# A decoder layer on one core: the SwiGLU's middle activations transposed by VectorE and moved by GpSimd's transfers

## The chip, the cores and the metric

The kernel runs on one core of a Trainium2 chip. The time is that of one execution on the device in microseconds; several executions are timed and their median is given.

## The reference

One layer with three residual parts over 256 positions of width 2048: a SwiGLU, a mixer (gated linear attention in 4 heads beside dilated attention in 8), and a second SwiGLU. All inputs are float32. The change touches the two SwiGLUs, which are the same but for their weights:

```python
def rms_norm(x, g):
    xf = x.astype(jnp.float32)
    y = xf * lax.rsqrt(jnp.mean(xf * xf, axis=-1, keepdims=True) + EPS)
    return (y * g.astype(jnp.float32)).astype(x.dtype)

def swiglu(x, w_gate, w_up, w_down):
    return (jax.nn.silu(x @ w_gate) * (x @ w_up)) @ w_down

x = x + FFN_RESIDUAL_WEIGHT * swiglu(rms_norm(x, ffn1_norm[l]), ffn1_w_gate[l], ffn1_w_up[l], ffn1_w_down[l])
...
x = x + FFN_RESIDUAL_WEIGHT * swiglu(rms_norm(x, ffn2_norm[l]), ffn2_w_gate[l], ffn2_w_up[l], ffn2_w_down[l])
```

`w_gate` and `w_up` are 2048 x 5632, `w_down` is 5632 x 2048.

## The kernel before

A float32 product is made of three products of rounded operands. `split` (line 87) cuts a tile in two: ScalarE copies it to the type float32r, which is the high part (line 89), and VectorE subtracts that from the tile, which leaves the low part (line 90). Weights become `wh` and `wl`, activations `hh` and `hl` (the normalised input) or `uh` and `ul` (the SwiGLU's middle activations). `products` (line 165) issues high by high (line 171), high by low (line 173) and low by high (line 175), and sums them in PSUM.

Weights come in loads of 1 MB from SyncE's queue (line 148) into one of three buffers `raw`. `prepare` splits each half of a load into a pair `wh`, `wl`, of which there are four buffers (`WBUF`), and `weights` keeps two or three pairs ahead of the matmuls. So the engines of a stage are tied in a ring: TensorE frees a weight buffer, ScalarE and VectorE fill it, VectorE frees the buffer `raw`, SyncE loads the next.

`column_pair` (line 183) is one stage: two blocks of 512 output columns (in the SwiGLU one of the gate and one of the up projection) for both halves of the positions (`t`, 128 each), so four PSUM banks out of six. It goes over the tiles `i` of the inner dimension, 16 in the up-projection and 44 in the down-projection, and for each over `t`; with two column blocks and three products that is 12 matmuls a tile. After the last tile of a half it calls `evac`. Small pieces of work are put in the list `later`, and `column_pair` runs them spread over the steps of the next stage.

In `ffn` (line 218) there are eleven up-projection pairs and then two down-projection pairs. `evac` (line 223) makes the middle activations of 512 columns and 128 positions: ScalarE takes the Silu of the gate (`sg`, line 225), VectorE multiplies it with the up part (`u`, line 226). `u` has positions in its partitions, but the down-projection needs the columns there, so TensorE transposes four squares of 128 into a PSUM bank `tb` (line 229, by the helper's line 85), and `split` writes `uh` and `ul` from that bank (line 230, shown as lines 89 and 90). The call is made twice in a pair, for `t` = 0 and 1.

A scheduler of the framework sets the order in which each engine gets its instructions; an engine then works through its own in that order, and an instruction that waits holds those behind it. GpSimd does small things only: powers for the normalisation (line 106), and loads of constants from its own DMA queue (lines 81 and 298 to 305).

Of the kernel before, what the change touches and what calls it, by code (L numbers as in the profile page):

```python
# [14 lines left out]
F32 = mybir.dt.float32  # L15
# [6 lines left out]
P = 128  # L22
S = 256
D = 2048
# [3 lines left out]
NT = S // P  # L28
# [8 lines left out]
def layer_kernel(tc, x, xT, gains, gla_gate_up, gla_gate_bias, gla_out_norm, att_q_norm, att_k_norm,  # L37
                 w_ff1, w_dn1, w_mix, w_low, w_out, w_ff2, w_dn2, c_sq, c_rope, c_mask, out):

    nc = tc.nc  # L40
# [3 lines left out]
    with ExitStack() as es:  # L44
        cst = es.enter_context(tc.tile_pool(name="cst", bufs=1))
# [7 lines left out]
        def t512(name):  # L53
            return cst.tile([P, 512], F32, name=name, tag="t512", bufs=4)

        def tp_bank():
            return ptp.tile([P, 512], F32, name="tp", tag="tp")


        xs = cst.tile([P, NT * D + 224], F32, name="xs")[:, :NT * D].rearrange("p (t d) -> p t d", t=NT)  # L60
        hh = cst.tile([P, KT, S], F32R, name="hh")
        hl = cst.tile([P, KT, S], F32R, name="hl")
        ident = cst.tile([P, P], F32, name="ident")
# [2 lines left out]
        ss = cst.tile([P, NT, 4], F32, name="ss")  # L66
        ssum = cst.tile([P, NT], F32, name="ssum")
        rt = cst.tile([P, NT], F32, name="rt")
        rq = cst.tile([P, 48], F32, name="rq")[:, :NT]
        junk = cst.tile([P, 512], F32, name="junk")  # L70

        nc.vector.memset(mhalf, -0.5)
# [10 lines left out]
        def transpose(dst, src):  # L83
            n = src.shape[0]
            nc.tensor.transpose(dst, src, ident[:n, :n])  # L85

        def split(dst_h, dst_l, src):

            nc.scalar.activation(dst_h, src, AF.Copy)  # L89
            nc.vector.tensor_sub(dst_l, src, dst_h.bitcast(F32))  # L90
# [71 lines left out]
        def halves(a):  # L162
            return a.rearrange("p (b a) -> p b a", b=2)
# [13 lines left out]
        later = []  # L177
# [5 lines left out]
        def column_pair(acts, evac, span=28, due=None, extra=None, final=False):  # L183

            ps = [None] * NT
            n = len(acts)  # L190
            total = done = 0
            i = 0
            while i < n:
                if i == due:
                    done += len(later)
                    run_later(len(later))
                if extra and i in extra:
                    extra[i]()
                g = WBUF if final and i == n - WBUF else 1
                ws = [weights() for _ in range(g)]  # L200
                for t in range(NT):
                    step = 2 * i + t
                    total = max(total, done + len(later))
                    go = max(-(-total * min(step + 1, span) // span) - done, 0)
                    done += min(go, len(later))
                    run_later(go)
                    if i == 0:
                        ps[t] = [acc_bank(), acc_bank()]
                    last = i + g == n
                    products(ps[t], t, acts[i:i + g], ws, i == 0, last, ((0,), (1,)) if g > 1 else ((0, 1),))  # L210
                    if last:
                        evac(t, [b.rearrange("p (a b) -> p b a", b=2) for b in ps[t]])
                i += g
# [4 lines left out]
        def ffn(name, done, extra=None, final=False):  # L218
            with tc.tile_pool(name=name, bufs=1, reuse_waits="tile") as fp:
                uh = fp.tile([P, FT, S], F32R, name="uh")  # L220
                ul = fp.tile([P, FT, S], F32R, name="ul")
                for b in range(FF // 512):
                    def evac(t, ps, b=b):
                        sg, u = t512("sg"), t512("u")
                        nc.scalar.activation(halves(sg), ps[0], AF.Silu, scale=rt[:, t:t + 1])  # L225
                        nc.vector.scalar_tensor_tensor(halves(u), ps[1], rt[:, t:t + 1], halves(sg), op0=ALU.mult, op1=ALU.mult)  # L226
                        tb = tp_bank()
                        for j in range(4):
                            transpose(tb[:, j * P:(j + 1) * P], u[:, j * P:(j + 1) * P])
                        split(uh[:, 4 * b:4 * b + 4, t * P:(t + 1) * P], ul[:, 4 * b:4 * b + 4, t * P:(t + 1) * P],  # L230
                              tb.rearrange("p (j q) -> p j q", j=4))
                    if b:
                        column_pair(hacts, evac)
                    else:
                        column_pair(hacts, evac, span=16, due=15 if extra else 8, extra=extra)
                for cp in range(2):
                    def evac(t, ps, cp=cp):
                        for j in range(2):
                            c = 2 * cp + j
                            blk = xs[:, t, c * 512:(c + 1) * 512]  # L240
                            nc.vector.scalar_tensor_tensor(halves(blk), ps[j], 0.5, halves(blk), op0=ALU.mult, op1=ALU.add)
                            done(t, c, blk)
                    column_pair([(uh, ul, k) for k in range(FT)], evac, final=final and cp == 1)
# [404 lines left out]
```

## Time and profile before

| what | value |
|---|---|
| median of 3 runs | 1795.85 us (1795.18 to 1795.98) |
| the profiled execution | 1795.97 us |
| its span, first to last instruction | 1794.0 us |
| mean granted TensorE clock, as a share of 2.4 GHz | 0.998 |
| bytes read from memory | 350.35 MB |
| TensorE, VectorE, ScalarE, GpSimd busy | 1783.4, 970.2, 840.6, 28.2 us |

A busy share says how long an engine worked, not whether the kernel waited for it. The chain of waits says that: it is followed back from the last instruction, at each step to what released it. In a timeline a row is an instruction, or several alike in a row, with its start, its duration, and in brackets the idle time before it and what ended that. A matmul's duration overlaps its neighbours', so the time that a matmul costs is read from the distance of starts.

### The profile page before, as it was taken

How to read it: one execution, taken by the hardware profiler on the slowest of the kernel's cores; microseconds unless marked ns; L12 is line 12 of the kernel's file. 1: busy time of each engine (PE TensorE's matmuls, PEld its weight loads, DVE VectorE, ACT ScalarE, POOL GpSimd, SP SyncE). 2: the span in 40 equal slices, each digit the busy share in tenths (PEclk: the TensorE clock that was granted, in tenths of full speed). 3: DMA queues.
4: the chain of work that ended last, by engine and by line, in shares of the span. 5: the costliest groups of instructions: out<-in, count | busy, mean ns of one | idle time of the engine just before them, and what ended most of it. 6: DMA issues, size and time to landing. Idle time of an engine off the chain costs nothing.

```text
span 1794.0 us, 20802 instructions
## 1 busy us (share of the span) xinstructions
PE 1783.4 (99%) x8462; PEld 1553.0 (87%) x8462; DVE 970.2 (54%) x998; ACT 840.6 (47%) x1012; POOL 28.2 (2%) x34
## 2 busy tenths in 40 slices
PE   8999999999999999999999999999999999999999
PEld 7888888888888888888887788888888888888887
DVE  5555555555544645566655666555555555544544
ACT  6444444444444544565753445444444444444342
POOL 0000000000000001011000000000000000000000
PEclk9999999999999999999999999999999999999999
DMA  8555555555555556555444455555555555555653
GB/s 330 190 210 190 207 190 205 193 190 208 199 201 210 188 211 206 195 204 194 165 165 151 153 189 191 208 191 208 189 208 191 207 190 205 194 208 194 232 205 124
DMA packets 52111, 353.79 MB, mean 197 GB/s; under 512 B 5904, under 2 KB 7952, under 8 KB 9776
## 3 DMA queue, kind: packets, MB, share of 16 engines
q1 hardware_dynamic: 48672, 348.15, 53.8%
q10 hardware_dynamic: 2896, 3.17, 0.6%
q0 software_dynamic: 448, 1.15, 0.2%
q8 instruction: 66, 1.08, 0.2%
q14 instruction: 29, 0.24, 0.0%
HBM read 350.35 MB, written 2.10 MB: 196 GB/s over the span
## 4 chain that ended last, share of the span: by engine, by line
PE 99%; ACT 1%; DMA 0%; DVE 0%; issue 0%; ACTq 0%
PE acc L171 32%; PE acc L173 31%; PE acc L175 31%; PE tp L85 2%; PE tp L512 0%; DMA xt<-in_xT_dram 0%; PE tp L378 0%; PE tp L527 0%; PE tp L530 0%; ACT wh L89 0%; ACT L445 0%; PE acc L432 0%; PE acc L433 0%; PE acc L434 0%; PE tp L404 0%
## 5 line engine op out<-in xcount | busy, mean ns | idle before, releaser
L90 DVE TENSOR_TENSOR wl<-raw,wh 128x1024 fp32r<-128x1024 f32 x658 | 802.8, 1224 | 693.6 <-ACT wh L89 693.4
L89 ACT ACTIVATE wh<-raw 128x1024 fp32r<-128x1024 f32 x658 | 691.9, 1055 | 791.1 <-PE acc L175 778.4
L173 PE MATMUL acc<-wl,hh 128*128 128x512 f32 x1792 | 549.2, 382 | 0.0
L175 PE MATMUL acc<-wh,hl 128*128 128x512 f32 x1792 | 543.9, 380 | 0.0
L171 PE MATMUL acc<-wh,hh 128*128 128x512 f32 x1792 | 538.5, 382 | 4.3 <-ACT wh L89 4.3
L171 PEld LDWEIGHTS acc<-wh,hh 128*128 128x128 f32 x1792 | 339.0, 190 | 52.8 <-ACT wh L89 4.6
L175 PEld LDWEIGHTS acc<-wh,hl 128*128 128x128 f32 x1792 | 338.6, 189 | 49.1 <-issue 2.1
L173 PEld LDWEIGHTS acc<-wl,hh 128*128 128x128 f32 x1792 | 338.6, 189 | 49.0 <-issue 2.0
L173 PE MATMUL acc<-wl,uh 128*128 128x512 f32 x704 | 212.6, 379 | 0.0
L175 PE MATMUL acc<-wh,ul 128*128 128x512 f32 x704 | 211.8, 379 | 0.0
L171 PE MATMUL acc<-wh,uh 128*128 128x512 f32 x704 | 210.8, 380 | 0.0
L175 PEld LDWEIGHTS acc<-wh,ul 128*128 128x128 f32 x704 | 133.1, 189 | 18.8
L173 PEld LDWEIGHTS acc<-wl,uh 128*128 128x128 f32 x704 | 133.1, 189 | 18.8
L171 PEld LDWEIGHTS acc<-wh,uh 128*128 128x128 f32 x704 | 133.0, 189 | 18.7
L90 DVE TENSOR_TENSOR ul<-tp,uh 128x512 fp32r<-128x512 f32 x44 | 29.6, 691 | 64.1 <-ACT uh L89 64.1
L89 ACT ACTIVATE uh<-tp 128x512 fp32r<-128x512 f32 x44 | 26.3, 597 | 79.1 <-PE tp L85 77.9
L225 ACT ACTIVATE sg<-acc,rt 128x512 f32<-128x512 f32 x44 | 30.2, 687 | 14.0 <-PE acc L175 13.4
L226 DVE SCALAR_TENSOR_TENSOR u<-acc,rt,sg 128x512 f32<-128x512 f32 x44 | 32.9, 747 | 2.8 <-ACT sg L225 0.4
L85 PE MATMUL tp<-ident,u 128*128 128x128 f32 x176 | 26.4, 273 | 0.0
L85 PEld LDWEIGHTS tp<-ident,u 128*128 128x128 f32 x176 | 22.0, 141 | 3.4
L106 POOL TENSOR_TENSOR rs<-a,mhalf 128x4 f32<-128x4 f32 (+1 forms) x12 | 17.4, 1454 | 278.9 <-DVE a L328 278.9
L171 PE MATMUL acc<-wh,oah 128*128 128x512 f32 x64 | 20.2, 385 | 0.0
(147 smaller groups left out, 558.7 us busy)
## 6 DMA issues: line engine op xcount, KB each, us to landing
raw<-in_w_ff_dram SPq DMA_DIRECT2D x175, 1024.0 KB, 4.8
raw<-in_w_dn_dram SPq DMA_DIRECT2D x88, 1024.0 KB, 4.8
raw<-in_w_mix_dram SPq DMA_DIRECT2D x48, 1024.0 KB, 4.8
raw<-in_w_out_dram SPq DMA_DIRECT2D x16, 1024.0 KB, 4.8
xt<-in_xT_dram ACTq DMA_DIRECT2D x8, 256.0 KB, 7.0
xs<-in_x_dram SPq DMA_DIRECT2D x2, 1024.0 KB, 9.5
raw<-in_w_ff_dram SPq DMA_DIRECT2D x4, 256.0 KB, 5.6
raw<-in_w_low_dram SPq DMA_DIRECT2D x1, 1024.0 KB, 4.7
```

The source lines that it names most:

```text
L85: nc.tensor.transpose(dst, src, ident[:n, :n])
L89: nc.scalar.activation(dst_h, src, AF.Copy)
L90: nc.vector.tensor_sub(dst_l, src, dst_h.bitcast(F32))
L106: nc.gpsimd.tensor_tensor(dst, src, mhalf[:, :src.shape[-1]], op=ALU.pow)
L171: nc.tensor.matmul(ps[j], lhsT=sh, rhs=alt(wh[:, j, :]), start=first and i == 0, stop=False)
L173: nc.tensor.matmul(ps[j], lhsT=sh, rhs=alt(wl[:, j, :]), start=False, stop=False)
L175: nc.tensor.matmul(ps[j], lhsT=sl, rhs=alt(wh[:, j, :]), start=False, stop=last and i == len(ws) - 1)
L225: nc.scalar.activation(halves(sg), ps[0], AF.Silu, scale=rt[:, t:t + 1])
L226: nc.vector.scalar_tensor_tensor(halves(u), ps[1], rt[:, t:t + 1], halves(sg), op0=ALU.mult, op1=ALU.mult)
```

## The change

After `u`, VectorE transposes squares of 32 columns by 32 positions within each group of 32 partitions and lays them out in `us` with the four 32-column pieces of each 128-square sorted by the partition group that they belong to. That leaves each square in the wrong group of partitions, and 16 transfers of GpSimd's queue, of 32 partitions by 128 columns (16 KB) each, put them in place in a new tile `ur`, of which there are two. `split` then reads `ur` instead of a PSUM bank. It is no longer called in `evac` but put in the list `later`, behind six empty entries for `t` = 0 and two for `t` = 1, so it runs in the next pair. Two paddings in SBUF, 896 and 128 bytes a partition, go.

```diff
-        xs = cst.tile([P, NT * D + 224], F32, name="xs")[:, :NT * D].rearrange("p (t d) -> p t d", t=NT)
+        xs = cst.tile([P, NT, D], F32, name="xs")
...
-        rq = cst.tile([P, 48], F32, name="rq")[:, :NT]
+        rq = cst.tile([P, 16], F32, name="rq")[:, :NT]
...
                         nc.vector.scalar_tensor_tensor(halves(u), ps[1], rt[:, t:t + 1], halves(sg), op0=ALU.mult, op1=ALU.mult)
-                        tb = tp_bank()
-                        for j in range(4):
-                            transpose(tb[:, j * P:(j + 1) * P], u[:, j * P:(j + 1) * P])
-                        split(uh[:, 4 * b:4 * b + 4, t * P:(t + 1) * P], ul[:, 4 * b:4 * b + 4, t * P:(t + 1) * P],
-                              tb.rearrange("p (j q) -> p j q", j=4))
+
+                        us = t512("us")
+                        ur = fp.tile([P, 512], F32, name="ur", tag="ur", bufs=2)
+                        nc.vector.transpose(us.rearrange("p (q j c) -> p j q c", q=4, j=4), u)
+                        for q in range(4):
+                            for r in range(4):
+                                nc.gpsimd.dma_start(ur[32 * q:32 * q + 32, r * P:(r + 1) * P],
+                                                    us[32 * r:32 * r + 32, q * P:(q + 1) * P])
+
+                        def finish():
+                            dst = [a[:, 4 * b:4 * b + 4, t * P:(t + 1) * P].rearrange("p j (q c) -> p j q c", q=4) for a in (uh, ul)]
+                            split(*dst, ur.rearrange("p (q j c) -> p j q c", q=4, j=4))
+
+                        later.extend([lambda: None] * (2 if t else 6) + [finish])
```

The orders below are those that the engines are given. A row is a line of the program, the operation, what it writes and reads, and its count.

TensorE, at the start of the second column pair, before the change (`u` and `tp` are the transposes' input and bank):

```order
L173 MATMUL acc<-wl,hh 128x512
L85 MATMUL tp<-ident,u 128x128 x4
L171 MATMUL acc<-wh,hh 128x512
L85 MATMUL tp<-ident,u 128x128 x4
L173 MATMUL acc<-wl,hh 128x512
L175 MATMUL acc<-wh,hl 128x512
```

and with it:

```order
L173 MATMUL acc<-wl,hh 128x512
L171 MATMUL acc<-wh,hh 128x512
L173 MATMUL acc<-wl,hh 128x512
L175 MATMUL acc<-wh,hl 128x512
```

The eight transposes are gone and the matmuls follow in the same order; the same holds in all 22 pairs.

ScalarE from one pair's Silu to the next pair's, before the change:

```order
L225 ACTIVATE sg<-acc,rt 128x512 x2
L89 ACTIVATE wh<-raw 128x1024
L89 ACTIVATE uh<-tp 128x4x128 x2
L89 ACTIVATE wh<-raw 128x1024 x15
L225 ACTIVATE sg<-acc,rt 128x512 x2
```

and with it:

```order
L225 ACTIVATE sg<-acc,rt 128x512
L89 ACTIVATE wh<-raw 128x1024
L225 ACTIVATE sg<-acc,rt 128x512
L89 ACTIVATE wh<-raw 128x1024 x7
L89 ACTIVATE uh<-ur 128x4x128
L89 ACTIVATE wh<-raw 128x1024 x6
L89 ACTIVATE uh<-ur 128x4x128
L89 ACTIVATE wh<-raw 128x1024 x2
L225 ACTIVATE sg<-acc,rt 128x512
```

The two `uh` now stand seven and thirteen weight tiles behind the second `sg`, instead of one, and one weight tile stands between the two `sg`. VectorE's order has `ul` and `wl` at the matching places, and its new transposes right behind each `u`.

GpSimd's queue from the start of the program, with the waits, before the change:

```order
L81 DMA ident<-in_c_sq_dram 128x128
L106 ISA
L106 TENSOR_TENSOR rt<-ssum,mhalf 128x1 [waits DVE_49] x2
L298 DMA rope<-in_c_rope_dram 128x2x128 [waits DVE_49,PE_49]
L299 DMA gq<-in_att_q_norm_dram 128x128
```

and with it (DMASW0 to DMASW7 are the semaphores of this queue's transfers):

```order
L81 DMA ident<-in_c_sq_dram 128x128
L106 ISA
L106 TENSOR_TENSOR rt<-ssum,mhalf 128x1 [waits DVE_49] x2
L233 DMA ur<-us 32x128 [waits DVE_49]
L233 DMA ur<-us 32x128 x6
L233 DMA ur<-us 32x128 [waits DMASW0_49]
L233 DMA ur<-us 32x128 [waits DMASW1_49]
L233 DMA ur<-us 32x128 [waits DMASW2_49]
```

352 transfers now stand ahead of the loads of line 298, and as many in the second SwiGLU. From the eighth on each waits for a semaphore of the queue's own, and they come round after eight.

## Rows read from the trace of the kernel before

**Rows 1.** The page's busy time, share of the span, instructions.

```profile
PE 1783.4 (99%) x8462; PEld 1553.0 (87%) x8462; DVE 970.2 (54%) x998; ACT 840.6 (47%) x1012; POOL 28.2 (2%) x34
```

**Rows 2.** The chain of waits, by line.

```profile
PE acc L171 32%; PE acc L173 31%; PE acc L175 31%; PE tp L85 2%; PE tp L512 0%; DMA xt<-in_xT_dram 0%; PE tp L378 0%; PE tp L527 0%; PE tp L530 0%; ACT wh L89 0%; ACT L445 0%; PE acc L432 0%; PE acc L433 0%; PE acc L434 0%; PE tp L404 0%
```

**Rows 3.** Windows: an up-projection pair, a down-projection pair; busy us of each engine.

```profile
112.30:154.62 42.32, 42.32 (x202) 37.09 (x200) 22.26 (x20) 19.15 (x20) 0.00 (x0) 1.00 0.54 198
...
1572.35:1686.31 113.96, 113.96 (x529) 99.79 (x529) 55.87 (x48) 46.34 (x44) 0.00 (x0) 1.00 0.59 212
```

**Rows 4.** Timelines: start, duration, instruction; ScalarE, VectorE, SyncE's queue, ScalarE.

```profile
93.49 1.06 ACT L89 ACTIVATE wh<-raw 128x1024 fp32r<-128x1024 f32 x1 [1.53 <-PE acc L175]
...
95.72 1.61 DVE L226 SCALAR_TENSOR_TENSOR u<-acc,rt,sg 128x512 f32<-128x512 f32 x2
...
120.02 0.33 SPq L148 DMA_DIRECT2D raw<-in_w_ff_dram  x1
...
130.63 1.06 ACT L89 ACTIVATE wh<-raw 128x1024 fp32r<-128x1024 f32 x1 [1.53 <-PE acc L175]
```

**Rows 5.** Waits for TensorE (total, times, longest), and for loads of `raw`.

```profile
ACT wh L89 <- PE acc L175: 778.4, 537, 4.8
...
  DMA raw<-in_w_ff_dram: 0.4, 1
```

**Rows 6.** Groups of instructions: shapes, count, busy us, mean ns, idle before.

```profile
L173 PE MATMUL acc<-wl,hh 128*128 128x512 f32 x1792 | 549.2, 382 | 0.0
...
L175 PE MATMUL acc<-wh,ul 128*128 128x512 f32 x704 | 211.8, 379 | 0.0
...
L90 DVE TENSOR_TENSOR ul<-tp,uh 128x512 fp32r<-128x512 f32 x44 | 29.6, 691 | 64.1 <-ACT uh L89 64.1
L85 PE MATMUL tp<-ident,u 128*128 128x128 f32 x176 | 26.4, 273 | 0.0
L89 ACT ACTIVATE uh<-tp 128x512 fp32r<-128x512 f32 x44 | 26.3, 597 | 79.1 <-PE tp L85 77.9
...
L255 DVE SCALAR_TENSOR_TENSOR hl<-xt,gT,hh 128x256 fp32r<-128x256 f32 x16 | 6.9, 480 | 6.8 <-ACT hh L254 6.8
```

**Rows 7.** TensorE's timeline at the start of a pair.

```profile
95.88 0.59 PE L171 MATMUL acc<-wh,hh 128*128 128x512 f32 x2
...
100.20 0.38 PE L173 MATMUL acc<-wl,hh 128*128 128x512 f32 x1
...
101.72 0.38 PE L175 MATMUL acc<-wh,hl 128*128 128x512 f32 x1
```

**Rows 8.** GpSimd's timeline, three of eight loads in a row.

```profile
709.18 0.54 POOL L301 DMA_DIRECT2D bm<-in_c_mask_dram  x1
709.71 0.54 POOL L302 DMA_DIRECT2D bm<-in_c_mask_dram  x1
710.23 0.54 POOL L303 DMA_DIRECT2D csq<-in_c_sq_dram  x1
```

**Rows 9.** DMA, 700 to 720 us: queue; issues with us to landing; `raw` over all.

```profile
q0 software_dynamic: 336, 0.82, 16.0%
...
gon<-in_gla_out_norm_dram POOLq DMA_DIRECT2D x1, 128.0 KB, 6.8
...
gq<-in_att_k_norm_dram POOLq DMA_DIRECT2D x1, 64.0 KB, 3.2
...
raw<-in_w_ff_dram SPq DMA_DIRECT2D x175, 1024.0 KB, 4.8
```

**Rows 10.** Timelines of GpSimd (two powers) and VectorE (two `wl`).

```profile
754.67 1.02 POOL L106 TENSOR_TENSOR rs<-a,mhalf 128x4 f32<-128x4 f32 x1 [40.53 <-DVE a L328]
760.24 2.52 POOL L106 TENSOR_TENSOR rs<-a,mhalf 128x4 f32<-128x4 f32 x1 [4.55 <-DVE a L328]
...
709.53 1.21 DVE L90 TENSOR_TENSOR wl<-raw,wh 128x1024 fp32r<-128x1024 f32 x1
...
760.67 1.22 DVE L90 TENSOR_TENSOR wl<-raw,wh 128x1024 fp32r<-128x1024 f32 x1
```

## The prediction

> **What bounds the kernel now.** The page's busy shares come first: TensorE works in 99% of the span [rows 1]. A share can hide a wait, so the chain of waits is next: the three matmul lines 171, 173 and 175 hold 32, 31 and 31% of it, and line 85, all the transposes of the program, 2% [rows 2]. So TensorE is the path, and what leaves it shortens the time unless something else becomes late. The windows show the stage that the change touches: one column pair of the up-projection (16 weight tiles, two token halves, 192 matmuls and eight transposes of `u`) takes 42.32 us, with VectorE busy 22.26, ScalarE 19.15, GpSimd nothing, the granted clock at 1.00 (its 2.4 GHz level) and the DMA engines at 0.54 [rows 3]. The second window is one column pair of the down-projection, 528 matmuls and no transposes: 113.96 us, or 0.2158 us a matmul.
>
> What is late next is the making of weights. ScalarE makes `wh` every 2.59 us and each time waits 1.53 us for TensorE to release a buffer [rows 4]; over the program it waits 778 us for TensorE, and for the weights' loads only 0.4 us [rows 5]. With four buffers a weight tile is begun when TensorE is done with the tile four places back, so 3 x 2.59 = 7.8 us lie before its use, and `wh` and `wl` need 1.06 + 1.22 = 2.3 of them [rows 4, 10].
>
> **What the change removes.** 176 transposes, eight in each of 22 column pairs. They are fp32 matmuls of 273 ns each, 26.4 us in all [rows 6], but they overlap their neighbours, so the price is read from starts: the matmul at 100.20 and the one at 101.72 stand three places apart without the transposes, and three matmuls at 0.2158 take 0.65, so the eight cost 1.52 - 0.65 = 0.87 us [rows 7]. The windows agree: 42.32 - 192 x 0.2158 = 0.88. The order of TensorE's matmuls is otherwise the same. 22 x 0.88 = **19.4 us** off the path.
>
> **What it adds on VectorE and ScalarE.** 44 transposes of 128x512. No row has one. From below it costs what 256 columns cost in a two-source operation, 0.48 us, from above what 1,024 columns cost, 1.22; the nearest is a 128x512 operation, 0.69 [rows 6, 10], which I take. Two in a pair make VectorE 23.6 of 41.4 us: hidden. `uh` and `ul` stay, at 0.60 and 0.69 from PSUM; from SBUF they can cost no more than `wh` and `wl` for twice the columns, 1.06 and 1.22, and I leave them as they are. `sg` of the second half now stands behind a `wh`, so its `u` is some 2 us later; its PSUM banks are wanted a whole pair later. Nothing on the path.
>
> **What it adds on GpSimd.** 704 transfers of 16 KB, 32 in a pair, where the queue was empty. The only rows with this queue in use are eight loads in the middle of the program: they are issued every 0.53 us, and land after 3.2 us, or after 6.8 where one met a burst of weight loads [rows 8, 9]. New is a wait: there are eight semaphores, so each transfer waits until the one eight places before it has landed, and behind it waits the rest of the queue. So one transfer costs max(0.53, landing/8) us: 0.53 at 3.2, 0.85 at 6.8.
>
> When must they be there? Count from the first matmul of the next pair, at 95.88 [rows 7]. `u` of the first half ends near 96.5 [rows 4], its transpose at 97.2, so transfers begin at +1.4. In ScalarE's order one `wh` (at +0.2, 2.59 after the one at 93.49) and seven more come before the first `uh`: ScalarE reaches it at 0.2 + 7 x 2.59 + 1.06 = +19.4; six more before the second: +34.9. ScalarE may be later than that by the slack of the buffers: the `wh` behind the first `uh` is the twelfth tile of its pair, used at 11 x 2.59 = +28.5, and `uh`, `wh`, `wl` take 3.0 before that, so the 16th transfer must have landed by +25.5; likewise the 32nd by 17 x 2.59 - 3.0 = +41.0. At 0.53 they land at 1.4 + 16 x 0.53 + 3.2 = +13.1 and +21.6. At 0.85, four rounds of 6.8, they land at +15.0 and +28.6. Both are before ScalarE even asks. TensorE waits only from 1.14 us a transfer (landing 3.2), or when a landing takes 39.6/4 = 9.9 us. With the load at 0.54 of the engines, I expect landings between the two rows, and no wait.
>
> **The weights' loads.** They share the 16 DMA engines. In the stretch with the eight loads GpSimd's queue took 16.0% of 16 engines for 20 us, 51 us for 0.82 MB, 6.4 us a transfer [rows 9]. By bytes 32 of ours (0.52 MB) take 33/16 = 2 us of the engines in a pair, by count 32 x 6.4/16 = 12.8 of 41.4: 5 to 31% on top of 54. A weight load is issued when `wl` frees its buffer (120.02) and used at 130.63, 10.6 us later, and lands after 4.8 [rows 4, 9]; longer by a third it is 6.5. Hidden at either end. The removed paddings (1 KB a partition) shift addresses and add no instruction.
>
> **Sum.** 1795.97 us, the profiled execution (span 1794.0 and 2.0 around it), less 19.4: 1776.6. It stands 0.1 above the median of the three runs, 1795.85, so the median becomes **1776.5** (span near 1774.6). Its own range is 1774 to 1779.
>
> **Rivals.**
> *GpSimd's issuing is held by VectorE (slower).* Against 0.53 stands this: the same power operation on GpSimd took 1.02 us beside small VectorE work and 2.52 when a `wl` ran into it [rows 10], 1.50 more. `wl` fills 1.22 of every 2.59 us; if it held a DMA issue in the same way, one would cost 0.53 + 0.47 x 1.50 = 1.24 on average, the 32nd transfer would land at 1.4 + 32 x 1.24 + 3.2 = +44.3, 3.3 us too late, and 22 x 3.3 = 73 us come on top: 1849; were every issue held, at 2.03, it is 28.6 a pair and some 2400. It decides from 1.14, and the gain is gone at 1.17. Against it: the issues at 709.18, 709.71 and 710.23 ran under the `wl` of 709.53 to 710.74 without losing their pace [rows 8, 10].
> The Trainium skill, "SBUF — State Buffer", sections "SBUF: two separate sides" and "Who interferes with whom", warns of this: VectorE's two-port operations shut GpSimd out of a shared port pair while it writes descriptors, and the page has a DMA of some 620 ns take some 3,100. It also says that an operation with two SBUF inputs, which `wl` is, blocks only GpSimd's reads. By the warning alone the time would be some 3150 us, an estimate from the page's 3.1 us a transfer; by its exception 1776.5, and the rows agree with the exception.
> *Matmuls loosen.* More small transfers, other addresses: the means of one matmul differ between 379 and 382 ns from stage to stage [rows 6], and 0.8% of 22 x 41.4 is 7 us: 1784. Against it: with 0.87 for the transposes the pace of the first window is (42.32 - 0.87)/192 = 0.2159, that of the second, where the DMA engines are busier, 0.2158 [rows 3].
> *TensorE was not what held these pairs.* Then the freed 0.88 becomes a wait for `wh` and the time stays 1796. Against it: ScalarE waits for TensorE in every tile [rows 4, 5].
>
> **How the numbers follow.** A run can tell 0.2%, 3.6 us, from no change. Forecast 0.77; held issue 0.13, since 0.53 is seen for eight transfers only, never in a queue with waits; looser matmuls 0.06; no change 0.04. Faster: 0.77 and most of the 0.06, 0.82; same 0.05; slower 0.13. The range takes in forecast and looser matmuls: 1774 to 1786.
>
> **What would show it.** Right: column pairs of 41.4 us, no line 85 with `u`, ScalarE's `uh` started without a wait, landings of `ur` under 9.9 us, GpSimd's issues near 0.5 to 0.85 us apart. Wrong: TensorE waiting for `wh` in the second half of a pair, ScalarE's `uh` waiting for transfers, or a pair still at 42.3.

## The result, and the profile after

| what | before | after |
|---|---|---|
| median | 1795.84 us (4 runs, 1795.18 to 1795.98) | 1776.38 us (4 runs, 1775.93 to 1776.61) |
| the profiled execution | 1795.97 us | 1776.39 us |
| its span | 1794.0 us | 1774.5 us |
| mean granted TensorE clock | 0.998 | 1.0 |

The ratio is 0.9893, with a 95% interval of 0.9877 to 0.9909: 19.5 us less, where 19.4 was worked out and 1776.5 forecast. Later, on another chip, the changed kernel took 1775.54, 1775.96 and 1776.28 us; one execution beside these took 2669.69 us at a mean clock of 0.655 and is left out here, as it is in the ratios.

The page of the changed kernel: busy time, GpSimd's DMA queue (packets, MB, share of 16 engines), and the chain of waits by line.

```profile
PE 1763.4 (99%) x8286; PEld 1534.8 (86%) x8286; DVE 995.3 (56%) x1042; ACT 839.4 (47%) x1012; POOL 372.4 (21%) x738
...
q0 software_dynamic: 22976, 12.73, 2.5%
...
PE 99%; ACT 1%; DMA 0%; DVE 0%; issue 0%; ACTq 0%
PE acc L171 32%; PE acc L173 32%; PE acc L175 32%; PE tp L85 1%; PE tp L521 0%; DMA xt<-in_xT_dram 0%; PE tp L387 0%; PE tp L536 0%; PE tp L539 0%; ACT wh L89 0%; ACT L454 0%; PE acc L441 0%; PE acc L443 0%; PE acc L442 0%; PE tp L413 0%
```

TensorE has 176 matmuls less than in [rows 1] and is still the path. Line 85 fell from 2% to 1% of the chain [rows 2]. GpSimd went from 28 to 372 us of work, and neither it nor its queue is in the chain: that a resource is 21% busy where it was 2% costs nothing as long as nobody waits for it.

A window of the changed kernel over one column pair of the up-projection, with the columns of [rows 3]:

```profile
93.47:134.91 41.44, 41.44 (x193) 36.29 (x192) 23.42 (x23) 19.10 (x21) 15.64 (x32) 1.00 0.62 214
```

Before it was 42.32 us with eight matmuls more. 0.88 us a pair, 22 pairs: 19.4.

Timelines of the changed kernel in the second column pair: its first matmul, and ScalarE:

```profile
94.77 0.59 PE L171 MATMUL acc<-wh,hh 128*128 128x512 f32 x2
...
113.10 1.06 ACT L89 ACTIVATE wh<-raw 128x1024 fp32r<-128x1024 f32 x1 [1.53 <-PE acc L175]
114.06 0.61 ACT L89 ACTIVATE uh<-ur 128x512 fp32r<-128x512 f32 x1
115.69 1.06 ACT L89 ACTIVATE wh<-raw 128x1024 fp32r<-128x1024 f32 x1 [1.01 <-PE acc L175]
...
129.60 0.61 ACT L89 ACTIVATE uh<-ur 128x512 fp32r<-128x512 f32 x1
131.23 1.06 ACT L89 ACTIVATE wh<-raw 128x1024 fp32r<-128x1024 f32 x1 [1.01 <-PE acc L175]
```

Neither `uh` has a bracket: ScalarE reached it and went on, 19.3 and 34.8 us after the first matmul. And the `wh` behind each waits 1.01 for TensorE, where most others wait 1.53, here as before [rows 4]: `uh` took 0.52 us out of a wait that was there anyway.

GpSimd's timeline over the same pair. The bracket of a row is the wait before it:

```profile
96.64 4.88 POOL L233 DMA_DIRECT2D ur<-us  x10 [22.62 <-ACT sg L225]
103.02 4.40 POOL L233 DMA_DIRECT2D ur<-us  x9 [1.50 <-DMA ur<-us]
107.69 0.50 POOL L233 DMA_DIRECT2D ur<-us  x1 [0.28 <-DMA ur<-us]
109.40 3.42 POOL L233 DMA_DIRECT2D ur<-us  x7 [1.21 <-DMA ur<-us]
113.53 2.49 POOL L233 DMA_DIRECT2D ur<-us  x5 [0.71 <-DMA ur<-us]
```

32 transfers from 96.64 to 116.02, 0.61 us each. The waits `<-DMA ur<-us` are those for the transfer eight places before. They cost 3.7 of the 19.4 us; 15.7 are issuing.

The tile `ur` over the whole program (ns min/median/max of an instruction; the last line is us from issue to landing):

```profile
L233 POOL DMA_DIRECT2D ur<-us x704: 496/496/553, 55.0 to 1562.9; - x176
L89 ACT ACTIVATE uh<-ur x44: 612/613/615, 72.6 to 1577.0; 128x512 fp32r<-128x512 f32 x44
...
  DMA ur<-us: 76.7, 62
...
DMA to landing us min/median/max: 1.6/3.8/6.4
```

No issue among 704 took over 0.553 us, and the only one that waited for a landing was GpSimd itself, 76.7 us in all. Two groups of VectorE:

```profile
L230 DVE STREAM_TRANSPOSE us<-u 128x512 f32<-128x512 f32 x44 | 31.3, 711 | 1.5
...
L90 DVE TENSOR_TENSOR ul<-ur,uh 128x512 fp32r<-128x512 f32 x44 | 30.1, 683 | 0.0
```

### The profile page after: what moved, and what is told of

It reads as the page before. It is cut to its first block, busy times and chain, and to the rows that moved or that the text cites. A ratio compares the mean times of both kernels' runs of the same rounds, so it can differ in the third digit from the quotient of the medians.

```text
span 1774.5 us, 21587 instructions
## 1 busy us (share of the span) xinstructions
PE 1763.4 (99%) x8286; PEld 1534.8 (86%) x8286; DVE 995.3 (56%) x1042; ACT 839.4 (47%) x1012; POOL 372.4 (21%) x738
## 3 DMA queue, kind: packets, MB, share of 16 engines
q8 instruction: 65, 1.06, 0.2%
## 4 chain that ended last, share of the span: by engine, by line
PE 99%; ACT 1%; DMA 0%; DVE 0%; issue 0%; ACTq 0%
PE acc L171 32%; PE acc L173 32%; PE acc L175 32%; PE tp L85 1%; PE tp L521 0%; DMA xt<-in_xT_dram 0%; PE tp L387 0%; PE tp L536 0%; PE tp L539 0%; ACT wh L89 0%; ACT L454 0%; PE acc L441 0%; PE acc L443 0%; PE acc L442 0%; PE tp L413 0%
## 5 line engine op out<-in xcount | busy, mean ns | idle before, releaser
L90 DVE TENSOR_TENSOR wl<-raw,wh 128x1024 fp32r<-128x1024 f32 x658 | 802.8, 1224 | 713.4 <-ACT wh L89 713.2
L233 POOL DMA_DIRECT2D ur<-us x704 | 344.2, 497 | 576.3 <-ACT sg L225 431.8
L230 DVE STREAM_TRANSPOSE us<-u 128x512 f32<-128x512 f32 x44 | 31.3, 711 | 1.5
L90 DVE TENSOR_TENSOR ul<-ur,uh 128x512 fp32r<-128x512 f32 x44 | 30.1, 683 | 0.0
L106 POOL TENSOR_TENSOR rt<-ssum,mhalf 128x1 f32<-128x1 f32 x6 | 3.9, 642 | 123.1 <-DVE ssum L110 123.0
```

The source lines that it names most:

```text
L106: nc.gpsimd.tensor_tensor(dst, src, mhalf[:, :src.shape[-1]], op=ALU.pow)
L230: nc.vector.transpose(us.rearrange("p (q j c) -> p j q c", q=4, j=4), u)
L233: nc.gpsimd.dma_start(ur[32 * q:32 * q + 32, r * P:(r + 1) * P], us[32 * r:32 * r + 32, q * P:(q + 1) * P])
```

## The experiments

The theory: TensorE bounds the pairs, so its 176 transposes are worth 0.11 us each, and all that takes their place is hidden, because the split asks for `ur` 19 and 35 us into the next pair. The rivals: the gain has another source (the paddings, other addresses); the path added costs something that the gain only outweighs; GpSimd's issuing is fragile beside VectorE.

### Where the gain comes from

**Only the paddings** removed from the kernel before:

```diff
-        xs = cst.tile([P, NT * D + 224], F32, name="xs")[:, :NT * D].rearrange("p (t d) -> p t d", t=NT)
+        xs = cst.tile([P, NT, D], F32, name="xs")
...
-        rq = cst.tile([P, 48], F32, name="rq")[:, :NT]
+        rq = cst.tile([P, 16], F32, name="rq")[:, :NT]
```

> The kernel before with the two paddings in SBUF taken out, as the change has them, and nothing else. My theory (the gain is the 176 transposes on TensorE): 1795.8 us, no change within 1 us. Rival (addresses matter, part of the gain is the paddings'): 1794 or less, and what is missing from 1795.8 is theirs.

Measured: 1795.38 us (10 runs), ratio 0.9999 (0.9990 to 1.0009). The paddings did nothing.

**The transposes put back** into the changed kernel, into a bank that nobody reads, beside the new path:

```diff
+                        tb = tp_bank()
+                        for j in range(4):
+                            transpose(tb[:, j * P:(j + 1) * P], u[:, j * P:(j + 1) * P])
```

> The changed kernel with TensorE's transposes of u issued again into a PSUM bank that nobody reads; VectorE's transposes, the transfers and the late split stay. My theory: the 0.88 us a pair come back, 22 x 0.88 = 19.4, so 1795.8 us (column pairs of 42.3). Rival (the gain is in VectorE's or ScalarE's order, or in the split that no longer waits for TensorE): it stays near 1776.

Measured: 1795.26 us (10 runs), ratio 0.9998 (0.9989 to 1.0008). A window over the same pair of that kernel:

```profile
93.90:136.20 42.30, 42.30 (x201) 37.07 (x200) 23.42 (x22) 19.09 (x20) 15.69 (x32) 1.00 0.60 212
```

GpSimd's 15.69 us are there, and the pair is back at 42.30. The whole gain is the transposes' time on TensorE.

**No transposition at all** in the kernel before; this leaves out the transposition of `u`:

```diff
-                        tb = tp_bank()
-                        for j in range(4):
-                            transpose(tb[:, j * P:(j + 1) * P], u[:, j * P:(j + 1) * P])
                         split(uh[:, 4 * b:4 * b + 4, t * P:(t + 1) * P], ul[:, 4 * b:4 * b + 4, t * P:(t + 1) * P],
-                              tb.rearrange("p (j q) -> p j q", j=4))
+                              u.rearrange("p (j q) -> p j q", j=4))
```

> The kernel before with the transposition of the middle activations left out: split reads u itself, no TensorE transposes, no VectorE transposes, no transfers. My theory: all that the change added is hidden, so this is no faster than the changed kernel, 1776.4 us within 1. Rival (the transfers and VectorE's transposes cost a little on the path, by contention for SBUF or the DMA engines): this one is faster than 1776.4 by what they cost.

Measured: 1776.30 us (1775.42 to 1776.80, 4 runs), ratio 0.9892 (0.9877 to 0.9906). A kernel that does nothing in place of the transposes is no faster than the changed one: the medians differ by 0.1 us, the runs of this kernel by 1.4, so 44 transposes on VectorE and 704 transfers cost nothing that these runs can tell.

### What hides the new path

**The split asked for early.** ScalarE's order is fixed so that the two `uh` stand one weight tile behind the second `sg`, where they stood before the change:

```diff
+        pinned = [False]
-        def split(dst_h, dst_l, src):
-            nc.scalar.activation(dst_h, src, AF.Copy)
+        def split(dst_h, dst_l, src, pin=False):
+            ins = nc.scalar.activation(dst_h, src, AF.Copy)
+            if pin:
+                tc.keep_in_program_order(ins)
...
-            split(wh, wl, raws[0][:, k])
+            split(wh, wl, raws[0][:, k], pinned[0])
...
-                        later.extend([lambda: None] * (2 if t else 6) + [finish])
+                        later.append(finish)
...
-                        column_pair(hacts, evac)
+                        pinned[0] = True
+                        column_pair(hacts, evac, due=1)
+                        pinned[0] = False
...
+                    pinned[0] = cp == 0
-                    column_pair([(uh, ul, k) for k in range(FT)], evac, final=final and cp == 1)
+                    column_pair([(uh, ul, k) for k in range(FT)], evac, due=1 if cp == 0 else None, final=final and cp == 1)
+                    pinned[0] = False
```

> The changed kernel with ScalarE's order pinned so that both uh stand where the kernel before has them, one weight tile behind the second sg, in front of the fifth weight tile of the pair. My theory: the late place of uh is what hides the transfers. The last of 32 lands near +24.5 us (issued by +21.2, landing 3.8), then uh, wh and wl take 2.9, so the fifth tile is ready at +27.4 and was needed at +10.4: TensorE waits 17 us a pair, 22 x 17 = 375 us, so about 2150 us. Rival (transfers cost little wherever they are asked for): below 1800.

Measured: 2103.87 us (one run), 327.5 more than the changed kernel, 14.9 a pair. Timelines of GpSimd, ScalarE and TensorE in that kernel, over one pair's start, and what the transfers took to land:

```profile
110.86 15.62 POOL L236 DMA_DIRECT2D ur<-us  x32 [39.59 <-ACT sg L228]
...
109.98 1.06 ACT L90 ACTIVATE wh<-raw 128x1024 fp32r<-128x1024 f32 x1
119.83 0.63 ACT L90 ACTIVATE uh<-ur 128x512 fp32r<-128x512 f32 x1 [8.79 <-DMA ur<-us]
127.64 0.63 ACT L90 ACTIVATE uh<-ur 128x512 fp32r<-128x512 f32 x1 [7.18 <-DMA ur<-us]
...
116.75 0.59 PE L178 MATMUL acc<-wh,hl 128*128 128x512 f32 x2
129.27 2.07 PE L174 MATMUL acc<-wh,hh 128*128 128x512 f32 x4 [11.93 <-ACT wh L90]
131.13 1.06 PE L176 MATMUL acc<-wl,hh 128*128 128x512 f32 x2
...
DMA to landing us min/median/max: 1.6/1.6/2.7
```

This is the chain that the change avoids: `uh` waits for its sixteen transfers, the `wh` behind it on ScalarE waits with it, and TensorE stops for 11.93 us. Two matmuls that took 0.59 before the stop take 1.06 after it. Windows of the same kernel, before, over and after the stop (the last three numbers are granted clock, DMA share and GB/s):

```profile
105.00:109.00 4.00, 4.00 (x21) 3.49 (x20) 1.41 (x2) 1.17 (x2) 0.00 (x0) 1.00 0.44 143
109.00:128.00 19.00, 8.34 (x39) 6.97 (x37) 4.43 (x6) 2.63 (x4) 15.62 (x32) 0.83 0.19 68
128.00:133.00 5.00, 3.73 (x9) 3.01 (x10) 4.44 (x5) 4.06 (x5) 0.00 (x0) 0.50 0.27 77
```

The clock is at 0.50, the 1.2 GHz level, when TensorE begins again. Matmuls wait 277.5 us for `wh` (`PE acc L174 <- ACT wh L90` in the list of waits, 23 times), where the changed kernel has one such wait, of 4.7: 272.8 more. TensorE's busy time grew by 54.7 (1818.1 against 1763.4), the same matmuls at the lower clock. The two are the 327.5 us. The wait is 12.4 us a pair where 17 were expected. The expectation had the transfers issued in some 19 us and landing after 3.8; here the 32 were issued in 15.62 without a wait and landed after 1.6. ScalarE stood still, so no weight buffers came free, and hardly a weight load was running (DMA share 0.19). The longer matmuls, 2.5 us a pair, were not expected.

**Twice the transfers**, of 64 columns instead of 128, and then **four times**, of 32; the bytes stay:

```diff
-                                nc.gpsimd.dma_start(ur[32 * q:32 * q + 32, r * P:(r + 1) * P],
-                                                    us[32 * r:32 * r + 32, q * P:(q + 1) * P])
+                                for k in range(0, P, 64):
+                                    nc.gpsimd.dma_start(ur[32 * q:32 * q + 32, r * P + k:r * P + k + 64],
+                                                        us[32 * r:32 * r + 32, q * P + k:q * P + k + 64])
```

> The changed kernel with each transfer cut in two of 64 columns: 64 in a pair, the same bytes. The scheduler puts uh further back by itself. My theory: a transfer costs its issue of 0.50 us or landing/8, whatever its size, so 64 take 32 to 39 us of GpSimd's queue in a pair of 41.4: still hidden, 1776 to 1790 us, GpSimd's issue twice as busy as in the changed kernel. Rival (the price is by bytes): the same time, but the queue no busier than with 32.

> The same with each transfer cut in four of 32 columns: 128 in a pair, the same bytes. My theory: 128 x 0.50 to 0.61 us = 64 to 78 us, more than the pair's 41.4, so GpSimd's queue becomes the path and the time is 1776 + 22 x (22.6 to 36.6) = 2270 to 2580 us, with TensorE waiting for wh behind a uh that waits for transfers. Rival (the price is by bytes): 1776.

Measured: 1785.0 us with 64 a pair (4 runs, ratio to before 0.9940, 0.9923 to 0.9956), 2376.19 us with 128 (one run). With 64, a window over a pair (columns as in [rows 3]):

```profile
1349.20:1390.64 41.44, 41.44 (x193) 36.28 (x193) 22.98 (x23) 19.11 (x21) 31.56 (x65) 1.00 0.63 216
```

The timelines of TensorE and ScalarE in the same kernel, where the first SwiGLU's first down-projection pair ends:

```profile
579.40 1.22 PE L171 MATMUL acc<-wh,uh 128*128 128x512 f32 x2 [1.97 <-ACT uh L89]
...
577.60 1.23 ACT L89 ACTIVATE hh<-hf 128x512 fp32r<-128x512 f32 x2
578.74 0.61 ACT L89 ACTIVATE uh<-ur 128x512 fp32r<-128x512 f32 x1
```

And two lines of its waits (who waited for whom: us in all, times, longest):

```profile
ACT uh L89 <- DVE xs L251: 5.9, 1, 5.9
...
PE acc L171 <- ACT uh L89: 4.5, 2, 2.5
```

GpSimd issues for 31.56 of 41.44 us and the pair is as long as with 32 transfers. For 9.7 more it waits for its own landings, so its queue is full in this pair; that this is still hidden goes with an `uh` that the scheduler set later than in the changed kernel. The 8.6 us over the changed kernel do not lie in such a pair. In this kernel's order the last `uh` of each SwiGLU stands behind the residual's work (`xs`), here also behind norm blocks' `hh`; TensorE waits for it twice, here for 1.97 us, and two matmuls then take 1.22 where two took 0.59. At neither place was a transfer waited for: the time went by a place in the order. The profiled span is 8.1 us longer: TensorE's waits grew by 4.5 in all, and its busy time by 3.7 (1767.1 against 1763.4). Why the scheduler put `uh` there stays open.

With 128 a pair, the tile `ur`:

```profile
L234 POOL DMA_DIRECT2D ur<-us x2816: 496/496/553, 54.3 to 2246.5; - x188
```

and lines of the waits:

```profile
DVE u L226 <- DMA ur<-us: 508.4, 33, 32.4
...
PE acc L171 <- DVE u L226: 448.3, 32, 29.0
PE acc L171 <- ACT uh L89: 88.4, 4, 24.3
```

An issue is 496 ns for 4 KB as it is for 16 KB. The price of this queue is by count, and 128 issues are 63.5 us in a pair of 41.4: GpSimd's queue has become the path. A pair is on average 41.4 + (2376.2 - 1776.4)/22 = 68.7 us, or 0.54 a transfer. The time came out as expected, but not by the wait that was expected (`wh` behind an `uh`): TensorE waited most, 448.3 us, for `u`, which frees its PSUM banks. By the program `sg`, `u` and `us` share four buffers, and `u` had to wait for transfers that still read `us`.

**The same transfers from SyncE's queue**, ahead of the weights' loads:

```diff
-                                nc.gpsimd.dma_start(ur[32 * q:32 * q + 32, r * P:(r + 1) * P],
-                                                    us[32 * r:32 * r + 32, q * P:(q + 1) * P])
+                                nc.sync.dma_start(ur[32 * q:32 * q + 32, r * P:(r + 1) * P],
+                                                  us[32 * r:32 * r + 32, q * P:(q + 1) * P])
```

> The changed kernel with the transfers issued on SyncE's queue, between the weight loads, instead of GpSimd's. My theory: an issue there takes 0.33 us, so 32 hold the queue for at least 10.7 us a pair (16 if landings of some 4 us over eight semaphores set the pace), while the weight loads behind them have only 5.8 us to spare: TensorE waits 5 to 10 us a pair, 1884 to 2000 us. Rival (a queue is as good as another): 1776.

Measured: 1991.81 us (one run), 215.4 more than the changed kernel, 9.8 a pair. The timelines of SyncE's queue and of ScalarE in that kernel:

```profile
106.88 20.71 SPq L233 DMA_DIRECT2D ur<-us  x32
127.69 26.85 SPq L148 DMA_DIRECT2D raw<-in_w_ff_dram  x8
...
118.13 0.63 ACT L89 ACTIVATE uh<-ur 128x512 fp32r<-128x512 f32 x1 [0.99 <-DMA ur<-us]
128.84 0.63 ACT L89 ACTIVATE uh<-ur 128x512 fp32r<-128x512 f32 x1 [10.07 <-DMA ur<-us]
132.72 2.00 ACT L89 ACTIVATE wh<-raw 128x1024 fp32r<-128x1024 f32 x2 [3.25 <-DMA raw<-in_w_ff_dram]
```

and a line of its waits:

```profile
PE acc L171 <- ACT wh L89: 170.8, 23, 8.2
```

One transfer takes 0.65 us here, little more than on GpSimd's queue. But for 20.71 us no weight load is issued, and the loads have 10.6 us of slack less a landing of 4.8 [rows 4, 9]. The queue is not all that differs, though: the scheduler also moved `uh`. Both stand four weight tiles behind the second `sg`, not seven and thirteen. So ScalarE stood 10.07 us at the second `uh` for its transfers, and the late load held the `wh` behind it 3.25 us longer. Of the 215.4 us, 166.1 are waits of matmuls for `wh` (170.8 less the 4.7 of the changed kernel), and TensorE's busy time grew by 49.1 (1812.5 against 1763.4). What SyncE's queue alone would cost, with `uh` in its late places, no run shows; that transfers ahead of loads delay these is what the rows show.

### Does VectorE hold GpSimd's issues?

**Copies on VectorE beside the transfers**: 320 copies of 128x512 from SBUF to SBUF, one a weight tile, whose result is not read:

```diff
+        copies = [False]
...
+                    if copies[0] and t == 0:
+                        nc.vector.tensor_copy(junk, xs[:, 1, 0:512])
...
+                        copies[0] = True
                         column_pair(hacts, evac)
+                        copies[0] = False
```

> The changed kernel with copies on VectorE put beside the transfers: 128x512 float32, SBUF to SBUF, one for each weight tile in the up-projections, some three in a row between two wl by the scheduler's order. The result of the copies is not read. My theory: GpSimd's issue stays at 0.50 us beside wl (two SBUF inputs), and the copies, which hold the second port, are the case in which VectorE could hold it; the time stays near 1776 us as long as a transfer costs under 1.14. Rival (VectorE never holds an issue): issues of 0.50 us beside the copies too. If copies do hold it: issues of 0.8 us or more where copies run, and 32 transfers taking 25 us or more instead of 19.4.

Measured: 1775.59 us (one run). The copies' group in that kernel (count, busy us, mean ns, idle before):

```profile
L213 DVE COPY junk<-xs 128x512 f32<-128x512 f32 x320 | 135.6, 424 | 5.7
```

and its tile `ur`:

```profile
L236 POOL DMA_DIRECT2D ur<-us x704: 496/496/756, 54.7 to 1561.1; - x176
```

The longest issue, on GpSimd, and the copy that ran into it, on VectorE:

```profile
103.46 0.76 POOL L236 DMA_DIRECT2D ur<-us  x1
...
103.70 0.42 DVE L213 COPY junk<-xs 128x512 f32<-128x512 f32 x1
```

The longest issue is 0.756 us, and the mean rose from 0.497 to 0.501. So copies do hold issues: 19 of the 704 took over 0.56 us, where in the changed kernel none did. In each of the 19 a copy had begun 0.06 to 0.24 us after the issue, and the issue ended 0.10 us after that copy, as in the two rows. Copies that began 0.27 us or later in an issue did not lengthen it. So the longest hold added 0.26 us, and the pace of the queue hardly changes. The Trainium skill, "SBUF — State Buffer", section "SBUF: two separate sides", names such copies as the ones that shut GpSimd out until the copy ends. The trace agrees on when a hold ends; it shows no fivefold time. What longer copies would do was not run.

### Can more be moved?

**Eight norm blocks too.** `norm_block` transposes `xs` for the next stage with four TensorE transposes. Here the blocks of the first two column groups, after the first SwiGLU and ahead of the second, go the way of `u` (32 transposes less):

```diff
...
+        spare = {}
+        def moved_block(t, c, gi):
+            us = t512("us")
+            ur = spare["ur"](t, c)
+            nc.vector.transpose(us.rearrange("p (q j c) -> p j q c", q=4, j=4), xs[:, t, c * 512:(c + 1) * 512])
...
+            nc.vector.tensor_mul(v, v, g)
+            split(*[a[:, 4 * c:4 * c + 4, t * P:(t + 1) * P].rearrange("p j (q c) -> p j q c", q=4) for a in (hh, hl)], v)
...
-            later.append(lambda: norm_block(t, c, gi))
+            later.append(lambda: (moved_block if c < 2 else norm_block)(t, c, gi))
...
```

> The changed kernel with eight blocks of the normalised input moved the same way: the blocks of the first two column groups, which are ready a whole down-projection or output stage before they are needed, are transposed by VectorE and moved by 16 transfers each. 32 more transposes leave TensorE. My theory: 32 x 0.11 = 3.5 us less, 1772.9 us, since a stage of 41 us or more hides them. Rival (the stage of w_out is too short beside the gated blocks' work, or the first projection of the next stage waits for hh): 1776 or more.

Measured: 1778.06 us (4 runs, 1777.27 to 1779.05; ratio to before 0.9902, 0.9887 to 0.9917), 1.7 more than the changed kernel instead of some 3 less. Timelines of ScalarE and TensorE in that kernel ahead of the second SwiGLU:

```profile
1087.53 1.23 ACT L89 ACTIVATE hh<-hf 128x512 fp32r<-128x512 f32 x2 [1.36 <-DVE hf L99]
1090.12 0.63 ACT L89 ACTIVATE hh<-qg 128x512 fp32r<-128x512 f32 x1 [1.36 <-DVE qg L286]
...
1090.81 1.22 PE L171 MATMUL acc<-wh,hh 128*128 128x512 f32 x2 [3.85 <-ACT hh L89]
```

The last moved block stands behind the norm blocks that TensorE still does, on VectorE and on ScalarE. The stage's first matmul waits 3.85 us for it, and two matmuls then take 1.22 us where two took 0.59 in the early split's rows. Its transfers were long over, the last issued at 1070.4 and no landing of these over 5.9 us: what came late was the multiplication by the norm's gain, which stood last on VectorE (`qg`). There is no next pair to hide in: the block is made right ahead of its use.

**Four blocks only**, those after the first SwiGLU, beside the changed kernel on the same chip; the edit is shown against the kernel with eight blocks:

```diff
-            later.append(lambda: (moved_block if c < 2 else norm_block)(t, c, gi))
+            later.append(lambda: (moved_block if c < 2 and gi == 1 else norm_block)(t, c, gi))
```

> The same computation as the changed kernel. Only the four norm blocks that follow the first SwiGLU pair's first two column groups are also transposed by VectorE and moved by transfers, so 16 fewer TensorE transposes than in the changed kernel; the blocks ahead of the second feed-forward, whose late tail cost a wait of 3.9 us in the run with eight blocks, stay with TensorE. My theory (a transpose taken off TensorE is worth 0.11 us wherever what replaces it arrives in time, and only the seam ate the gain of the earlier run): 16 times 0.11 is 1.8 us less than the changed kernel, 1774.0 to 1775.2. Rival (the moved norm blocks are late here too, or something else follows TensorE's shorter work): 1776.0 or more.

> The changed kernel once more, beside the run with four blocks on the same chip: 1776.0 to 1776.8, so that a difference of 1 to 2 us between the two can be read.

Measured: 1773.90 us (1773.36 to 1774.85, 4 runs; ratio to before 0.9882, 0.9867 to 0.9897), and the changed kernel 1775.54 to 1776.28 (three runs; 0.9894, 0.9874 to 0.9914). The two intervals overlap, the single runs do not: some 2 us less, a tenth of a per cent, with 16 transposes less (1.8 by their price; the median is 0.1 under what was expected). One matmul group in the middle of the program (the attention's scores, an instruction's ns, first and last start), in the changed kernel and in this one:

```profile
L387 PE MATMUL tp<-kT,qT x32: 273/378/383, 842.9 to 892.3; 128*128 128x128 f32 x16, 128*128 128x256 f32 x16
```

```profile
L403 PE MATMUL tp<-kT,qT x32: 272/378/382, 840.7 to 890.2; 128*128 128x128 f32 x16, 128*128 128x256 f32 x16
```

The 2.2 us are won before 843 us, where the four blocks are, and the spans differ by the same 2.2 (1773.8 and 1771.6). The kernel with eight blocks was at 840.7 too, and lost 3.9 us after it. This is the fastest version that was run.

## Why the prediction was right

- **TensorE is the path.** It was, and still is: 99% of the chain. With nothing in place of the transposes the time is the same 1776.3.
- **176 transposes, 0.88 us a pair.** The pair went from 42.32 to 41.44, and putting them back brings 42.30. That the price was read from the distance of starts and not from 273 ns each was what mattered: by durations the gain would have been 48 us.
- **VectorE's transpose, 0.69 us.** It takes 0.711, and VectorE is busy 23.42 us in a pair, where 23.6 was said. `uh` and `ul`, left at 0.60 and 0.69, take 0.613 and 0.683.
- **GpSimd's transfers.** Landings were to lie between 3.2 and 6.8 us: the median is 3.8. The rule max(0.53, landing/8) gives 0.53 for 3.8; the pair's 32 took 0.61 each. Issuing is 0.49, and landings over 8 x 0.49 = 3.9 us, the longest 6.4, hold the queue, as the price at 6.8 had it. The transfers begin at +1.9 us and not +1.4: 0.54 pass between VectorE's end of the transpose, at 96.10, and the first issue, which the working left out. Both misses were too small to reach the slack. The last issue ends at +21.3, and with the longest landing all is there by +27.6, inside the +21.6 to +28.6.
- **When ScalarE asks.** +19.4 and +34.9 were said, +19.3 and +34.8 are in the timeline. The early split shows what this is worth: 327 us.
- **The DMA engines.** By bytes the transfers were to add 2 us of the engines in a pair, by count 12.8. The queue's 2.5% of 16 engines over 1774.5 us are 710 us, 1.0 a transfer, 2.0 a pair: the price by bytes. The 6.4 us a transfer of [rows 9] were not those of this kind of transfer. Weight loads land after 4.9 us, before 4.8 (a third more would have been 6.4, not the 6.5 of the working; nothing hangs on it).
- **The rivals.** VectorE's `wl` does not hold the issues: 704 of them between 0.496 and 0.553 us, beside `wl` in every tile. Copies hold some, by 0.26 us at most. The matmuls did not loosen: 41.44/192 = 0.2158. TensorE was what held the pairs.
- **What would decide.** The working put the point at 1.14 us a transfer for 32 of them, 36 us of queue in a pair. 64 transfers, 31.6 us of issuing and a full queue, left the pair at 41.44; 128, 63.5 us, did not. In both the scheduler had also moved `uh`, so the runs bound the point from both sides only loosely, and none tests it in the changed kernel's order.

The size of the range was not put to the test: the four runs stayed within 0.6 us of the forecast, the three later ones within 1.0.

## What to carry to other kernels

Where TensorE is the path, a transpose on it costs what the distance of starts says (0.11 us here), and it can be replaced by something some twenty times slower (19.4 us of transfers where eight transposes took 0.88), if its reader asks a stage later; read from the timeline when the reader asks, and place the reader so. A queue of small transfers is priced here by its count, and its place is a queue on which nothing urgent stands behind it. Where the result is wanted right ahead of a stage, as in the norm blocks, one wait can lose more than the transposes were worth (3.85 us against 1.8), even with the transfers long over: the order of the work behind them has to be read too.

## What was not expected of the hardware

- The same 16 KB transfer lands after 1.6 us where hardly a weight load is running (the early split), after 3.8 where they run all the time, and after 1.8 from SyncE's queue while that queue issues no loads. The Trainium skill, "DMA: Bandwidth & Descriptors", section "Anatomy of one DMA", has some 2.0 us plus the bytes for a transfer of this queue; the rows of GpSimd's queue lie on both sides of that.
- GpSimd's issue takes 496 ns for 16, 8 and 4 KB alike; SyncE's 507 to 1632, with a median of 589.
- After stops of 3.85 us (eight blocks) and 11.93 us (early split) the next matmuls come 0.43 us apart instead of 0.22, in both at a granted clock of 0.50. A wait of TensorE costs more than its length: in the early split 272.8 us of added waits came with 54.7 us of longer matmuls.
